# Seven-product pairs chained in two PSUM banks with held tails, three adds a pair, four weight splits, and closing products in two stretches of k tiles

## The chip, the cores and the metric

One program runs on one NeuronCore of a Trainium2 chip. The metric is the device time of one execution in microseconds (us); lower is better. The engines are TensorE (PE), VectorE (DVE), ScalarE (ACT), GpSimd (POOL) and SyncE (SP, which issues most transfers). Each works through its own queue in order and waits on semaphores for the others.

## The reference

One layer of a trunk for 128 context and 512 latent tokens (640 columns in all), width 1024, in fp32. Cut to what matters here:

```python
def swiglu(h, w_gate, w_up, w_down):
    return (jax.nn.silu(h @ w_gate) * (h @ w_up)) @ w_down      # inner width 2816

def trunk_layer(x, mod, ...):
    h = modulate(rms_norm(x, norm_ffn1), sh1, sc1)
    x = x + 0.5 * gt1 * swiglu(h, w_ffn1_gate, w_ffn1_up, w_ffn1_down)
    h = modulate(rms_norm(x, norm_mix), sh2, sc2)
    x = x + gt2 * mixer(h, ...)    # sigmoid gates; Fourier and gated linear attention branches; @ w_out
    h = modulate(rms_norm(x, norm_ffn2), sh3, sc3)
    x = x + 0.5 * gt3 * swiglu(h, w_ffn2_gate, w_ffn2_up, w_ffn2_down)
```

## The kernel before

Activations lie transposed, 128 channels on the partitions and 640 tokens along the row, cut in halves of `NH` = 320. Every fp32 operand is split in a high and a low part: `split` has ACT write the high part (L107) and DVE the rest (L108), and each product of two tiles becomes three matmuls (high by high, high by low, low by high).

**Pairs.** The gate and up projections of both FFNs, the mixer's branch gates and the projection of the attention output go through `Pair7`: a pair of 128-wide output tiles by two halves of 320 tokens, as a 2x2 scheme with seven products of half size in place of eight. Product i takes weights i, which are a quarter of the raw tile or a sum of quarters, and one of seven sums of activations that `Act7` has made. The four weight sums are made in place by POOL (L474, L477, L481, L485); `weights` splits seven pieces of 128x512. `product` runs 12 matmuls of 320 columns (L502) into a PSUM bank of its own. A `Take` object puts the seven products together: one copy on ACT (L529) and seven adds on DVE (L530 to L545). `done` of a gate pair applies silu (L556), that of an up pair multiplies on POOL (L566) and splits the result into a page of the hidden activation.

**Buffers.** `wraw` has two raw weight tiles, `wspl` ten blocks for split weights, `pb` six PSUM banks. A split waits until the last matmul that read its block is through; a transfer waits until POOL and the splits have left the raw tile.

**Stages, in order.** FFN1: an entry (three plain products and one pair, the pair's sums of activations made meanwhile by DVE and POOL, L436 and L440), then pairs in four parts of 4, 6, 6, 6 hidden tiles; after each part `down` (`gemm_w`, L138) adds its share of the down projection, one pair into the next part. Until about 325 us the weights of the modulation are streamed between the pairs (L214). The last part goes through `halved` (L392): eight output tiles by two halves, each a run over all k tiles, with the norm that follows hooked behind each tile. Then the mixer: an entry with two plain gate products (their sigmoids, `first_gate`, L1096, free the PSUM banks), a `turn` of transposes (L1045, copies L1048), gate pairs; Fourier and attention; `plain` (L1216), the branch's projection by pairs (`TakeY`), and `halved` with w_out. FFN2 is as FFN1, without the stream.

A scheduler decides at build time in which order each engine's queue holds the instructions; it is shown below from the built programs.

## Time and profile before

| | before |
|---|---|
| median of 3 runs | 1557.94 us (1556.88 to 1559.18) |
| the profiled execution | 1558.36 us, span 1556.6 us |
| mean granted TensorE clock | 0.984 |
| PE, DVE, ACT, POOL busy | 96%, 71%, 44%, 28% |
| instructions | 28126, of which 11162 matmuls |

The span is the time from the first to the last instruction on the core; some 1.8 us of the execution lie around it. The clock of 0.984 is a mean: 1 is 2.4 GHz, and 0.5 is 1.2 GHz, the lower of the two levels.

### The profile page before, as it was taken

How to read it: one execution, taken by the hardware profiler on the slowest of the kernel's cores; microseconds unless marked ns; L12 is line 12 of the kernel's file. 1: busy time of each engine (PE TensorE's matmuls, PEld its weight loads, DVE VectorE, ACT ScalarE, POOL GpSimd, SP SyncE). 2: the span in 40 equal slices, each digit the busy share in tenths (PEclk: the TensorE clock that was granted, in tenths of full speed). 3: DMA queues.
4: the chain of work that ended last, by engine and by line, in shares of the span. 5: the costliest groups of instructions: out<-in, count | busy, mean ns of one | idle time of the engine just before them, and what ended most of it. 6: DMA issues, size and time to landing. Idle time of an engine off the chain costs nothing.

```text
span 1556.6 us, 28126 instructions
## 1 busy us (share of the span) xinstructions
PE 1495.9 (96%) x11162; PEld 1457.1 (94%) x11162; DVE 1098.4 (71%) x2027; ACT 689.6 (44%) x1397; POOL 432.2 (28%) x320
## 2 busy tenths in 40 slices
PE   6989999999999999999989998989989999999998
PEld 5889999999999899999979998989989999999997
DVE  6876764675577876666668868887787674674676
ACT  5533342343345555464545454335643442442344
POOL 2432431441440000001054424310253532532510
PEclk7999999999999999999999999999999999999999
DMA  9383563522134512213124336354213222222232
GB/s 360 108 299 123 186 238 119 190 68 96 55 108 145 158 41 76 68 45 109 51 68 133 95 107 208 107 197 162 83 55 109 82 82 82 82 82 83 75 102 108
DMA packets 149338, 184.61 MB, mean 119 GB/s; under 512 B 4735, under 2 KB 121847, under 8 KB 149207
## 3 DMA queue, kind: packets, MB, share of 16 engines
q1 hardware_dynamic: 149207, 182.81, 35.7%
q8 instruction: 88, 1.44, 0.4%
q14 instruction: 43, 0.35, 0.1%
HBM read 168.64 MB, written 14.16 MB: 117 GB/s over the span
## 4 chain that ended last, share of the span: by engine, by line
PE 75%; DVE 11%; ACT 4%; issue 4%; DMA 2%; POOL 2%; SPq 1%; POOLq 0%; ACTq 0%; DVEq 0%
PE pb L502 34%; PE pb L138 16%; PE pb L392 7%; PE mm L834 4%; DVE wspl L108 3%; PE mm L138 2%; DVE pg L108 2%; PE sc L983 2%; PE sm L214 2%; ACT wspl L107 1%; DMA wraw<-in_w_in_dram 1%; PE sm L834 1%; PE pb L130 1%; ACT pg L107 1%; PE sm L1013 1%
## 5 line engine op out<-in xcount | busy, mean ns | idle before, releaser
L502 PE MATMUL pb<-pg,wspl 128*128 128x320 f32 x4452 | 667.2, 311 | 20.3 <-ACT g L1096 6.3
L502 PEld LDWEIGHTS pb<-pg,wspl 128*128 128x128 f32 x4452 | 658.2, 189 | 25.8 <-DVE wspl L108 6.9
L108 DVE TENSOR_TENSOR wspl<-wraw,wspl 128x512 fp32r<-128x512 f32 (+1 forms) x619 | 459.1, 759 | 235.3 <-ACT wspl L107 234.4
L107 ACT ACTIVATE wspl<-wraw 128x512 fp32r<-128x512 f32 (+1 forms) x619 | 359.3, 603 | 475.3 <-PE pb L138 155.3
L138 PE MATMUL pb<-pg,wspl 128*128 128x320 f32 x1920 | 288.8, 311 | 5.2 <-DVE pg L1216 5.0
L138 PEld LDWEIGHTS pb<-pg,wspl 128*128 128x128 f32 x1920 | 284.0, 189 | 6.9 <-DVE pg L1216 5.6
L474 POOL TENSOR_TENSOR wraw<-wraw 128x512 f32<-128x512 f32 x53 | 72.3, 1364 | 354.5 <-DVE wspl L108 352.0
L392 PE MATMUL pb<-pg,wspl 128*128 128x320 f32 (+2 forms) x960 | 149.8, 315 | 8.9 <-ACT pg L107 8.5
L392 PEld LDWEIGHTS pb<-pg,wspl 128*128 128x128 f32 x960 | 143.8, 192 | 10.5 <-ACT pg L107 9.4
L481 POOL TENSOR_TENSOR wraw<-wraw 128x512 f32<-128x512 f32 x53 | 69.8, 1318 | 165.4 <-DVE wspl L108 165.4
L108 DVE TENSOR_TENSOR pg<-t,pg 128x640 fp32r<-128x640 f32 (+2 forms) x64 | 60.3, 950 | 40.3 <-ACT pg L107 39.7
L834 PE MATMUL mm<-wspl,pg 128*128 128x256 f32 x672 | 87.8, 286 | 0.1
L107 ACT ACTIVATE pg<-t 128x640 fp32r<-128x640 f32 (+2 forms) x64 | 41.7, 663 | 100.6 <-POOL t L566 91.5
L834 PEld LDWEIGHTS mm<-wspl,pg 128*128 128x128 f32 x672 | 82.4, 191 | 0.7 <-ACT pg L936 0.4
L477 POOL TENSOR_TENSOR wraw<-wraw 128x512 f32<-128x512 f32 x53 | 81.9, 1546 | 4.1
L566 POOL TENSOR_TENSOR t<-t,g 128x640 f32<-128x640 f32 x40 | 63.7, 1605 | 63.0 <-DVE t L540 56.6
L485 POOL TENSOR_TENSOR wraw<-wraw 128x512 f32<-128x512 f32 x53 | 70.5, 1331 | 4.2
L372 DVE SCALAR_TENSOR_TENSOR pg<-pb,hg,pg 128x320 f32<-128x320 f32 x144 | 54.4, 433 | 19.0 <-PE pb L138 19.0
L1035 POOL TENSOR_TENSOR rs<-ms,negh 128x5 f32<-128x5 f32 x4 | 4.8, 1200 | 206.9 <-DVE ms L1033 206.9
L108 DVE TENSOR_TENSOR pg<-pg,pg 128x320 fp32r<-128x320 f32 (+2 forms) x80 | 58.3, 775 | 0.2 <-ACT pg L107 0.2
L138 PE MATMUL mm<-pg,wspl 128*128 128x320 f32 x288 | 52.3, 326 | 0.0
L130 PE MATMUL pb<-pg,wspl 128*128 128x320 f32 x288 | 47.2, 321 | 4.2 <-ACT wspl L107 2.9
(211 smaller groups left out, 1542.0 us busy)
## 6 DMA issues: line engine op xcount, KB each, us to landing
pg<-in_w_ada_dram SPq DMA_DIRECT2D x72, 512.0 KB, 7.5
wraw<-in_w_ffn_down_dram SPq DMA_DIRECT2D x32, 768.0 KB, 4.6
wraw<-in_w_ffn_gate_dram SPq DMA_DIRECT2D x22, 1024.0 KB, 5.2
wraw<-in_w_ffn_up_dram SPq DMA_DIRECT2D x22, 1024.0 KB, 5.2
wraw<-in_w_in_dram SPq DMA_DIRECT2D x22, 512.0 KB, 3.8
wraw<-in_w_in_dram SPq DMA_DIRECT2D x10, 1024.0 KB, 5.1
wraw<-in_w_out_dram SPq DMA_DIRECT2D x8, 1024.0 KB, 5.5
gbd<-g SPq DMA_DIRECT2D x16, 320.0 KB, 2.4
```

The lines of the kernel that those rows point to most:

```text
L107: S.activation(out=hi, in_=src, func=AF.Copy)
L108: eng.tensor_tensor(out=lo, in0=src, in1=hi.bitcast(F32), op=ALU.subtract)
L130: T.matmul(out=bank(ps, hf)[:, 0:NH], lhsT=w[a][k], rhs=acts[k][:, b, hf * NH:(hf + 1) * NH], start=(k == 0 and ti == 0), stop=(k == nk - ...
L138: T.matmul(out=bank(ps, hf)[:, 0:NH], lhsT=w[a][k], rhs=acts[k][:, b, hf * NH:(hf + 1) * NH], start=(k == 0 and ti == 0), stop=(k == nk - ...
L392: T.matmul(out=ps[:, 0:c1 - c0], lhsT=w[a][i], rhs=acts[i][:, b, c0:c1], start=(i == 0 and ti == 0), stop=(i == nk - 1 and ti == 2))
L474: G.tensor_tensor(out=self.a11, in0=self.a11, in1=self.a21, op=ALU.subtract)
L477: G.tensor_tensor(out=self.a21, in0=self.a21, in1=self.a22, op=ALU.add)
L481: G.tensor_tensor(out=self.a22, in0=self.a22, in1=self.a11, op=ALU.subtract)
L485: G.tensor_tensor(out=self.a12, in0=self.a12, in1=self.a22, op=ALU.subtract)
L502: T.matmul(out=self.p[i], lhsT=self.w[i][:, s, k, :], rhs=x[k][:, t, :], start=(k == 0 and ti == 0), stop=(k == self.n - 1 and ti == 2))
L566: G.tensor_tensor(out=x, in0=x, in1=g, op=ALU.mult)
L834: T.matmul(out=ps_out, lhsT=h2[k][:, a, t * P:(t + 1) * P], rhs=w[b][k], start=(k == 0 and ti == 0), stop=(k == KD - 1 and ti == 2))
```

## The change

A pair's products go into two banks that accumulate several products each: product 1 opens bank A, and 6, 7 and 4 are added to it by the matmuls themselves; product 5 opens bank B, and 3 is added to it; product 2 has a bank of its own. Between two products ACT copies what the bank holds so far (`p1`, `p16`, `p167`). Three adds on DVE are left (`p2`, `p5`, `p53`). The order of a pair is now 1, 2, 6, 5, 7, and its products 3 and 4 are held back (`held`) until the next pair: 3 runs behind that pair's 2, and 4 behind its 5. Where no pair follows, `flush_pair` runs them behind the first product of what comes next.

Weights are split in three pieces of 128x1024 (weights 1 and 2; 7 and 5; 6 and 3) and one of 128x512 (4), in four double blocks (`wspl2`) and two single ones, which take the room that the ten had. All other splits of weights go in pieces of up to 1024 too. A pair's sums stand in two steps: two sums, the split of 7 and 5, two sums, the split of 6 and 3.

`halved` runs the first four tiles of its first half over all k tiles but the last two, runs the held tails behind the first of them, and then closes the four. At the two FFN entries and the mixer's entry the calls for weights and activation sums stand in another order.

```diff
-NBLK = 10
+NBLK = 2
+NBLK2 = 4
...
+    def block2():
+        uid[0] += 1
+        return wspl2.tile([P, 2, 1024], F32R, tag="wspl2", name=f"wsplb{uid[0]}")
+
-    def wsplit(src, new=block, room=512):
+    def wsplit(src, new=block2, room=1024):
...
         for hf, c0, c1 in ((0, 0, cut), (1, cut, N)):
+            opened = []
             for mp in range(4):
                 rd = load(wd, r0, nk, mp * 256, 256)
                 for m in range(2):
                     w = wsplit(rd[:, :, m * P:(m + 1) * P])
...
+                    ps = pb_ps()
+                    if hf == 0 and mp < 2:
+                        some(ps, w, c0, c1, range(nk - 2))
+                        opened.append((2 * mp + m, ps, w))
+                        flush_pair()
+                        continue
+                    some(ps, w, c0, c1, range(nk))
+                    close(2 * mp + m, ps, hf, c0, c1)
+                if mp == 1:
+                    for k, ps, w in opened:
+                        some(ps, w, c0, c1, range(nk - 2, nk))
+                        close(k, ps, hf, c0, c1)
...
+            if i in (1, 2):
+                self.double(self.raw[:, :, 0:P], 1, 2, whole)
+            elif i in (5, 7):
+                self.weights(1)
+                G.tensor_tensor(out=self.a11, in0=self.a11, in1=self.a21, op=ALU.subtract)
+                G.tensor_tensor(out=self.a21, in0=self.a21, in1=self.a22, op=ALU.add)
+                self.double(self.raw[:, self.ks[0], :], 7, 5, lambda j, o: (j, o * P))
+            elif i in (6, 3):
+                self.weights(7)
+                G.tensor_tensor(out=self.a11, in0=self.a22, in1=self.a11, op=ALU.subtract)
+                G.tensor_tensor(out=self.a12, in0=self.a12, in1=self.a11, op=ALU.subtract)
+                self.double(self.raw[:, :, 0:P], 6, 3, whole)
...
         def begin(self):
-            self.product(1)
-            self.product(2)
-            self.take.c11(self.p[1], self.p[2])
+            self.A, C = pb_ps()[:, 0:NH], pb_ps()[:, 0:NH]
+            self.product(1, self.A, True)
+            self.take.p1(self.A)
+            self.product(2, C, True)
+            self.take.p2(C)
+            flush_step()
 
         def end(self):
-            self.product(7)
-            self.product(4)
-            self.product(6)
-            self.take.uv(self.p[6], self.p[7])
-            self.take.c21(self.p[4])
-            self.product(5)
-            self.take.c22(self.p[5])
-            self.product(3)
-            self.take.c12(self.p[3])
+            self.product(6, self.A, False)
+            self.take.p16(self.A)
+            self.B = pb_ps()[:, 0:NH]
+            self.product(5, self.B, True)
+            flush_step()
+            self.product(7, self.A, False)
+            self.take.p167(self.A)
+            self.take.p5(self.B)
+            held.extend((self.tail3, self.tail4))
...
+        def p16(self, ps):
+            self.w = sm_tile([P, NH], "sqh")
+            S.activation(out=self.w, in_=ps, func=AF.Copy)
...
+        def p53(self, ps):
+            self.last = V.tensor_tensor(out=self.x0[:, NH:N], in0=self.w, in1=ps, op=ALU.add)
+            self.done(0)
...
                 pd = out_ps()
                 gemm_w(pd, w, hid)
+                flush_pair()
...
-                    pair.sum(5)
+                    pair.weights(7)
                     act.each(act.sum4)
-                    pair.weights(7)
+                    act.each(act.put2)
+                    pair.weights(6)
+                    pair.begin()
+                    act.each(act.put1)
+                    t = swiglu(p[2], pu)
+                    keep(t, hid)
                     act.each(act.put4)
                     pair.weights(4)
...
             pair.weights(7)
-            act.each(act.put4)
-            pair.weights(2)
+            act.each(act.put2)
+            pair.weights(6)
         first_gate(m)
     turn()
+    pair.begin()
+    act.each(act.put1)
+    act.each(act.put4)
     pair.weights(4)
-    pair.begin()
-    act.each(act.put2)
-    pair.weights(6)
-    act.each(act.put1)
-    pair.weights(5)
     pin(m2)
     pair.end()
```

ACT's queue at the mixer's entry, before: from the split of weights 7 (`wspl_8620`) to the sigmoids of the second gate product (L1096); `pg_` are splits of activation sums.

```order
L107 ACTIVATE wspl_8620<-wraw_8494 128x512
L107 ACTIVATE pg_8470<-pg_8454 128x320
L107 ACTIVATE pg_8470<-pg_8455 128x320
L107 ACTIVATE pg_8471<-pg_8456 128x320
L107 ACTIVATE pg_8471<-pg_8457 128x320
L107 ACTIVATE wspl_8631<-wraw_8494 128x512
L1096 ACTIVATE g_8634<-pb_8566 128x320
L1096 ACTIVATE g_8634<-pb_8567 128x320
```

The same place of the changed kernel: `wsplb_8184` is the split of weights 7 and 5, `wsplb_8197` that of 6 and 3, L1161 the sigmoids.

```order
L109 ACTIVATE wsplb_8184<-wraw_8057 128x1024
L109 ACTIVATE pg_8035<-pg_8023 128x320
L109 ACTIVATE pg_8036<-pg_8024 128x320
L109 ACTIVATE pg_8037<-pg_8025 128x320
L109 ACTIVATE pg_8038<-pg_8026 128x320
L109 ACTIVATE wsplb_8197<-wraw_8057 128x1024
L1161 ACTIVATE g_8200<-pb_8129 128x320
L1161 ACTIVATE g_8200<-pb_8130 128x320
```

The sigmoids stood behind a split of raw weights 2; they now stand behind that of 6 and 3, which needs all four sums of the pair.

PE's queue at the entry of FFN2, before: the end of product 2 of the first pair (`wspl_12099`), product 7 (`wspl_12173`) and the start of product 4 (`wspl_12184`).

```order
L502 MATMUL pb_12214<-pg_11602,wspl_12099 128x320 x3
L502 MATMUL pb_12251<-pg_12074,wspl_12173 128x320 x3
L502 MATMUL pb_12251<-pg_12075,wspl_12173 128x320 x3
L502 MATMUL pb_12251<-pg_12076,wspl_12173 128x320 x3
L502 MATMUL pb_12251<-pg_12077,wspl_12173 128x320 x3
L502 MATMUL pb_12264<-pg_12078,wspl_12184 128x320 x6
```

Now: the end of product 2 (`wsplb_11398`), product 6 (`wsplb_11485`, the split of 6 and 3) and the start of product 5 (`wsplb_11468`).

```order
L537 MATMUL pb_11489<-pg_10931,wsplb_11398 128x320 x3
L537 MATMUL pb_11488<-pg_11376,wsplb_11485 128x320 x3
L537 MATMUL pb_11488<-pg_11377,wsplb_11485 128x320 x3
L537 MATMUL pb_11488<-pg_11378,wsplb_11485 128x320 x3
L537 MATMUL pb_11488<-pg_11379,wsplb_11485 128x320 x3
L537 MATMUL pb_11561<-pg_10885,wsplb_11468 128x320 x3
```

The third product of the entry's pair is now one whose weights need all four sums; before it was one that needs the first alone.

POOL's queue in FFN2 between a gate pair and an up pair, before: the sums of the up pair's weights (`wraw_13128`, L474 and L477, L481 and L485) and the two multiplications of the up pair ahead of it (L566).

```order
L474 TENSOR_TENSOR wraw_13128<-wraw_13128 128x4x128
L477 TENSOR_TENSOR wraw_13128<-wraw_13128 128x4x128
L566 TENSOR_TENSOR t_12893<-t_12893,g_12501 128x640
L566 TENSOR_TENSOR t_12892<-t_12892,g_12500 128x640
L481 TENSOR_TENSOR wraw_13128<-wraw_13128 128x4x128
L485 TENSOR_TENSOR wraw_13128<-wraw_13128 128x4x128
```

Now, for an up pair (`wraw_12578`) in the same place: sums L517, L518, L522, L523, multiplications L629 (half a row) and L634.

```order
L629 TENSOR_TENSOR t_12354<-t_12354,g_12229 128x320
L517 TENSOR_TENSOR wraw_12578<-wraw_12578 128x4x128
L634 TENSOR_TENSOR t_12353<-t_12353,g_12228 128x640
L518 TENSOR_TENSOR wraw_12578<-wraw_12578 128x4x128
L522 TENSOR_TENSOR wraw_12578<-wraw_12578 128x4x128
L523 TENSOR_TENSOR wraw_12578<-wraw_12578 128x4x128
```

The whole-row multiplication now stands between the first and the second sum; the split of 7 and 5 needs both.

## Rows read from the trace of the kernel before

**Rows 1.** Page, busy time by engine: us, share of the span, instructions.

```profile
PE 1495.9 (96%) x11162; PEld 1457.1 (94%) x11162; DVE 1098.4 (71%) x2027; ACT 689.6 (44%) x1397; POOL 432.2 (28%) x320
```

**Rows 2.** The chain of waits by time: start, us, what ran.

```profile
1205.32 73.92 PE pb L502 x504
```

**Rows 3.** Waits of PE: line, awaited engine and line, us in total, times, longest.

```profile
PE pb L392 <- ACT pg L107: 8.5, 3, 3.9
PE pb L502 <- ACT g L1096: 6.3, 1, 6.3
PE pb L502 <- DVE wspl L108: 5.5, 4, 1.8
PE pb L138 <- DVE pg L1216: 5.0, 2, 4.6
PE pb L502 <- ACT g L578: 3.4, 2, 2.1
PE pb L502 <- DVE hn L533: 3.2, 2, 2.9
```

**Rows 4.** Windows, PE alone: window, us, busy us (instructions), granted clock, DMA share, GB/s.

```profile
464.00:472.00 8.00, 5.67 (x39) 1.00 0.33 100
809.60:813.60 4.00, 3.97 (x15) 0.52 0.74 250
850.00:858.00 8.00, 5.06 (x24) 0.79 0.46 139
961.00:971.00 10.00, 5.01 (x21) 0.66 0.13 44
1037.00:1050.00 13.00, 8.72 (x38) 0.74 0.87 320
```

**Rows 5.** Groups by form: line, shapes, count, busy us, mean ns, idle before.

```profile
L108 DVE TENSOR_TENSOR wspl<-wraw,wspl 128x512 fp32r<-128x512 f32 x555 | 426.1, 785 | 233.7 <-ACT wspl L107 233.0 <-issue 0.3
L107 ACT ACTIVATE wspl<-wraw 128x512 fp32r<-128x512 f32 x555 | 333.8, 625 | 441.1 <-PE pb L138 141.7 <-POOL wraw L481 106.1 <-PE pb L502 72.1
L533 DVE TENSOR_TENSOR hn<-hn,pb 128x320 f32<-128x320 f32 x53 | 25.5, 480 | 17.3 <-PE pb L502 17.2
L529 ACT ACTIVATE hn<-pb 128x320 f32<-128x320 f32 x53 | 22.6, 426 | 15.6 <-PE pb L502 15.5
L942 DVE TENSOR_TENSOR pg<-pg,pg 128x1280 f32<-128x1280 f32 x4 | 6.0, 1493 | 23.9 <-ACT pg L941 23.9
L941 ACT ACTIVATE pg<-pg 128x1280 f32<-128x1280 f32 x4 | 5.1, 1274 | 0.1
L474 POOL TENSOR_TENSOR wraw<-wraw 128x512 f32<-128x512 f32 x53 | 72.3, 1364 | 354.5 <-DVE wspl L108 352.0 <-DVE mod L221 2.5
L477 POOL TENSOR_TENSOR wraw<-wraw 128x512 f32<-128x512 f32 x53 | 81.9, 1546 | 4.1
L566 POOL TENSOR_TENSOR t<-t,g 128x640 f32<-128x640 f32 x40 | 63.7, 1605 | 63.0 <-DVE t L540 56.6 <-DVE t L545 4.2 <-ACT wspl L107 2.2
```

**Rows 6.** Timelines of PE, POOL and DVE at the mixer's entry: start, us, work, idle before.

```profile
809.63 6.67 PE L502 MATMUL pb<-pg,wspl 128*128 128x320 f32 x32 [6.27 <-ACT g L1096]
...
799.11 6.30 POOL L440 TENSOR_TENSOR pg<-pg 128x320 f32<-128x320 f32 x4 [3.05 <-DVE pg L436]
...
806.72 1.27 POOL L477 TENSOR_TENSOR wraw<-wraw 128x512 f32<-128x512 f32 x1
812.60 1.76 POOL L481 TENSOR_TENSOR wraw<-wraw 128x512 f32<-128x512 f32 x1 [4.62 <-DVE wspl L108]
...
801.70 1.36 DVE L108 TENSOR_TENSOR wspl<-wraw,wspl 128x512 fp32r<-128x512 f32 x1
...
810.06 0.68 DVE L108 TENSOR_TENSOR wspl<-wraw,wspl 128x512 fp32r<-128x512 f32 x1
```

**Rows 7.** Timelines of PE and POOL at the entry of FFN2.

```profile
1133.52 3.68 PE L502 MATMUL pb<-pg,wspl 128*128 128x320 f32 x24
...
1133.36 4.51 POOL L440 TENSOR_TENSOR pg<-pg 128x320 f32<-128x320 f32 x4 [2.37 <-DVE pg L436]
```

More of the change, by code (lines that the diff above doesn't have):

```diff
@@ L373, in add_gated, with halved @@
                                    in1=X[k][:, a:b], op0=ALU.mult, op1=ALU.add)
-    def halved(wd, r0, acts, gate, X, each, mid, cut=NH):
-        nk = len(acts)
+    def halved(wd, r0, nk, acts, gate, X, each, mid, cut=NH):
         late = []
@@ L381, in flush, with some, close @@
                 late.pop(0)()
+        def some(ps, w, c0, c1, ks):
+            for i in ks:
+                for ti, (a, b) in enumerate(((0, 0), (0, 1), (1, 0))):
+                    T.matmul(out=ps[:, 0:c1 - c0], lhsT=w[a][i], rhs=acts[i][:, b, c0:c1],
+                             start=(i == 0 and ti == 0), stop=(i == nk - 1 and ti == 2))
+        def close(k, ps, hf, c0, c1):
+            flush()
+            for r, a, b in ((0, c0, min(c1, NL)), (1, NL, c1)):
+                if a < b:
+                    V.scalar_tensor_tensor(out=X[k][:, a:b], in0=ps[:, a - c0:b - c0], scalar=gate[:, k, r:r + 1],
+                                           in1=X[k][:, a:b], op0=ALU.mult, op1=ALU.add)
+            late.append(lambda: each(k, hf))
+            if hf == 1 and k in mid:
+                late.append(mid[k])
         for hf, c0, c1 in ((0, 0, cut), (1, cut, N)):
+            opened = []
             for mp in range(4):
@@ L489, in weights, with product @@
                 return
-            self.sum(i)
-            self.w[i] = self.block()
-            src = {1: self.a11, 2: self.a12, 3: self.a12, 4: self.a22, 5: self.a21, 6: self.a22, 7: self.a11}[i]
-            split(self.w[i][:, 0], self.w[i][:, 1], src)
-        def product(self, i):
+            whole = lambda j, o: (range(2 * self.n)[self.ks[o]][j], 0)
+            if i in (1, 2):
[10 more added lines that the diff above has]
+                self.double(self.raw[:, :, 0:P], 6, 3, whole)
+            else:
+                t = block()[:, :, 0:self.n * P]
+                v = [t[:, s].rearrange("p (k c) -> p k c", k=self.n) for s in range(2)]
+                split(v[0], v[1], self.a22)
+                self.w[4] = [[v[s][:, j, :] for j in range(self.n)] for s in range(2)]
+        def product(self, i, bank, first):
             self.weights(i)
@@ L549, in out, with p1674, p53 @@
             return [sm_tile([P, N], self.tag) for _ in range(2)]
-    class TakeGate(Take):
+    class TakeAct(Take):
         tag = "g"
+        def p1674(self, ps):
+            S.activation(out=self.x1[:, 0:NH], in_=ps, func=self.func)
+            S.activation(out=self.x1[:, NH:N], in_=self.x1[:, NH:N], func=self.func)
+            self.done(1)
+        def p53(self, ps):
+            self.last = V.tensor_tensor(out=self.x0[:, NH:N], in0=self.w, in1=ps, op=ALU.add)
+            S.activation(out=self.x0, in_=self.x0, func=self.func)
+            self.done(0)
+    class TakeGate(TakeAct):
+        func = AF.Silu
         def done(self, i):
-            x = self.x1 if i else self.x0
-            S.activation(out=x, in_=x, func=AF.Silu)
+            pass
     class TakeUp(Take):
@@ L652, in ffn @@
             if f0 + nf == DFF // P:
-                halved(wd, f0 * P, hid, gate, X, each, mid, cut)
+                halved(wd, f0 * P, nf, hid, gate, X, each, mid, cut)
                 break
```

147 lines of the change are left out of this document (65 added, 82 removed).

## The prediction

> **What bounds the kernel now.** The page comes first: PE is busy for 1495.9 us of the span [rows 1], and no other engine comes near. The chain of waits tells what undisturbed work costs: 504 matmuls of a pair's kind in 73.92 us [rows 2], or 0.147 us each. A product of 12 is 1.76 us, a pair of 84 is 12.3 us. The change leaves the number of matmuls alone (seven products of 12 for each pair, the closing tiles only cut in two), so time can come or go only where PE waits or runs at the lower clock. The waits of PE name the places [rows 3]; the windows show where the clock fell beside them [rows 4].
>
> The reader is to see two things there. Inside the FFN stages there is no wait of weight on the list: all named ones lie at entries and at closings. And the clock falls after some waits and not after others: 464 to 472 us, with a wait of 2.3 us, keeps 1.00, while the windows round the waits of 2.9, 3.9, 4.6 and 6.3 us show 0.52 to 0.79. At 0.52 PE is at 1.2 GHz nearly throughout. I take it that a wait of up to 2.3 costs itself, and one from 2.9 up about 2 us more.
>
> **What the change should give.** *Closings (L392).* Three waits, 8.5 us, the longest 3.9 [rows 3], so the other two are 2.3 each. The two of 2.3 lie at the FFN closings, the long one at w_out. In the changed kernel PE has, when it gets there, the first tile over all but two k tiles, then the held products 3 and 4 (3.5 us), then three tiles more before it needs the last two. With six k tiles these three are 3 x 12 matmuls = 5.3 us, with w_out's eight 3 x 18 = 7.9 us. That is more than each wait. At w_out the clock goes back too: 0.74 over 13 us is 3.4 us lost [rows 4]. 2.3 + 2.3 + 3.9 + 3.4 = 11.9, and I take 11.5, since the last hidden tiles now come later by the held products. The last sums there are not on the list of anything else.
>
> *The wait for `plain`'s add (L1216).* 4.6 us of its 5.0, with the clock at 0.66 over 10 us. That is 3.4 us by the window, but PE worked only half of it, so about 2 is real. The held products of the gate pair put 3.5 us of PE work ahead of it and the rest, about 1.1, is too short for a fall. Gain 3.5 + 2 = 5.5.
>
> *The wait for the add L533 among the gate pairs.* 2.9 us, and 0.79 over 8 us, which is 1.7 us. DVE is what is late here. It loses four adds of 0.48 us a pair [rows 5], 1.9 us, and the splits get no dearer. Most of 4.6 should go: 3.5.
>
> Sum of the gains: 20.5 us.
>
> **What each new operation costs.** A DVE split of 1024 columns isn't in the trace. From below: the two-input instruction of 1280 columns, 1.49 us [rows 5], by 1024/1280 is 1.19. From above: two splits of 512 at the slowest row, 1.36 each [rows 6], or 2.7. I take 1.22, near the lower end, since an undisturbed 512 is 0.68 [rows 6] and the longer instruction saves one start. On ACT the bounds are 1.02 (1.27 for 1280) and 1.25 (two of 0.625) [rows 5]; I take 1.06. The two new copies of a bank are 0.43 each, as L529; ACT is busy for 44% [rows 1] and hides them, unless they stand behind something that waits (below). Per pair DVE goes from 7 x 0.785 + 7 x 0.48 = 8.9 us to some 3 x 1.22 + 0.785 + 3 x 0.48 = 5.9. It is hidden work in the FFN stages, so worth nothing there by itself. Of the other splits in larger pieces I expect nothing either way: the attention stage has no wait of PE on the list that a split ends. Bounds: 2 us more or less.
>
> **What it should take.** *Mixer's entry.* PE now waits 6.27 us for the second gate's sigmoids and goes on at 809.63 [rows 6]. These now stand behind the split of 6 and 3, as the order shows. POOL ends the activation sums at 799.11 + 6.30 = 805.4; two weight sums of 1.27 take it to 808.0; the split of 7 and 5 ends at 809.1 on ACT and 810.3 on DVE; two more sums 812.9; the split of 6 and 3 on ACT 814.0; two sigmoids at some 0.4, 814.8. Product 1 then starts 5.2 us later than now. The clock has fallen already now, so no more is lost by it. I count 5.2.
>
> *Both FFN entries.* Now they cost PE 5.5 + 3.4 us together (the waits for L108's blocks and for L578) [rows 3], 4.45 each. In the new order product 6 is third. In FFN2 products 1 and 2 end at 1133.52 + 3.68 = 1137.2, POOL's activation sums at 1133.36 + 4.51 = 1137.9 [rows 7]. Behind these stand the last two weight sums, 2.8 us, and the split: ACT 1141.8, DVE 1143.0, which the third matmul needs. PE waits 5.8 us in place of 4.45, and that is long enough for a fall of the clock, which now doesn't come: 4.0 us at 0.52 [rows 4] lose 1.9. So 3.2 more at each, 6.4 for both, if FFN1's entry goes as FFN2's.
>
> *The FFN pairs.* A block of 1 and 2 comes free when product 2 ends, and from there runs a chain: ACT split 1.06, DVE 1.22, the two sums 1.36 and 1.55 [rows 5], ACT split of 7 and 5 1.06. Where an up pair is followed by a gate pair, ACT's queue has the copy `p16` of the running pair behind that split, and product 7 waits for the copy: 0.43 more, 6.7 in all with 0.1 for the start 6.8. PE in that time has products 3, 6, 5 and 4, 7.04 us. It fits by 0.2. But in the cycle before, POOL does the whole-row multiplication, 1.6 us [rows 5], between the two sums (the order above). The up pair's split of 6 and 3 then ends on ACT at 12.9 us after the gate pair's product 2, past the end of the up pair's own product 2 at 12.3; the next split starts 0.6 late on ACT, and is 1.1 late on DVE, where that of 6 and 3 (1.22) comes first. Less the slack of 0.2, product 7 is some 0.9 to 1.0 late. There are eight such places that neither the modulation's stream nor a down projection covers (two in FFN1, six in FFN2): 8 us.
>
> Sum of the losses: 5.2 + 6.4 + 8 = 19.6 us.
>
> **The sum.** The profiled execution took 1558.36 us, 0.4 above the median. 1558.4 - 20.5 + 19.6 = 1557.5; as to the median, about 1557. The two large sums cancel; each has its own uncertainty.
>
> **The rivals.**
> *The chain fits* (0.32). If the splits of 7 and 5 and of 6 and 3 take their lower bounds and the sums the undisturbed 1.27 [rows 6], the delay in the cycle before shrinks by about 0.9 and product 7 waits for nothing. For it: in the FFN stages PE waits for nothing now, and DVE has a third less to do. Against: the order puts three engines in one chain with 0.2 us of slack. The 8 us are not paid: 1549.
>
> *The chain is too long for every pair* (0.20), the other side. POOL and DVE slow each other when both work: L481 took 1.76 at 812.60 against 1.27 undisturbed, and a split on DVE 1.36 against 0.68 [rows 6]. If the DVE split of 1024 comes to 1.9, half way to double, both on the way (1 and 2; 6 and 3) add 0.7, so the eight places pay 2.4 each, 19 us, and eight transitions with no multiplication between pay about 0.5, 4 us. That is 15 more than the forecast: 1572. It decides from a split of about 1.5. The Trainium skill, page "SBUF — State Buffer", section "Who interferes with whom", says that VectorE and GpSimd share one pair of ports as an exclusive lock, so that an instruction of the one holds off the other to its end; a split with two SBUF inputs is of that kind, and a longer one would hold POOL's sums for longer. The rows of contention agree with it; how far a piece of 1024 is hit no run here shows yet.
>
> *The held work does not fill the waits* (0.10). If the held products come to a place where the engine behind them was late anyway, the results that the closings wait for are late by the same 3.5 us, and only half of the 20.5 comes: 1567.
>
> **How the numbers follow.** The forecast itself, the cancelling, has 0.38 and a range of its own of 1551 to 1563 (the terms are good to some 3 us each). 0.2%, about what a measurement of this kernel can tell from no change, is 3.1 us, so 1554.8 to 1561.1 counts as no change. Faster: the first rival 0.32 and 0.10 of the forecast's 0.38. No change: 0.20 of it. Slower: its last 0.08, and the other two rivals with 0.30. The range of 1546 to 1576 goes 3 below the first rival and 4 above the second.
>
> **What would show it.** Right: PE's waits at the two FFN closings gone, and the one at w_out gone with its window back at 1.00; the wait at the mixer's entry longer, some 11 us, still ended by the sigmoids (L1161); at the FFN entries a wait of near 6 us for the split of 6 and 3; in FFN2 waits of about 1 us ahead of product 7, ended by the copy L582, and DVE near a third less busy. Wrong: no waits at L582, or many more than eight; a split of 1024 above 1.5 us on DVE; a wait at the closings that comes back as one for the held products' results; a gate stage that still waits for DVE.

## Result and the profile after

The changed kernel takes 1597.26 us (median of 4, 1594.64 to 1598.31) against 1557.41 for the kernel before: 1.0254 times as long [1.0235, 1.0274]. The forecast was 1557, with a range up to 1576. The profiled execution is the one of 1598.31 us, with a span of 1596.5 us, a mean granted clock of 0.977 and 27071 instructions.

The page first, its line of busy times:

```profile
PE 1507.8 (94%) x11162; PEld 1463.5 (92%) x11162; DVE 995.3 (62%) x1544; ACT 692.4 (43%) x1253; POOL 419.0 (26%) x320
```

The number of matmuls is unchanged, DVE is busy for 9% less [rows 1] where the forecast looked for near a third, and PE is busy for 12 us more in a span 40 us longer: it ran longer at the lower clock and it waited more. PE's waits, the longest groups:

```profile
engine line waited for: us in total, times, longest us
PE pb L537 <- ACT hn L575: 13.7, 3, 6.0
PE pb L537 <- ACT g L1161: 12.0, 1, 12.0
PE pb L537 <- DVE g L589: 11.7, 11, 3.1
...
PE pb L537 <- ACT sqh L582: 5.0, 3, 2.3
PE pb L537 <- ACT wsplb L109: 3.4, 3, 1.9
PE pb L391 <- DVE wsplb L110: 3.4, 1, 3.4
```

L537 is `product`, as L502 was. Of the waits of before [rows 3], those for L533, for `plain`'s add and at the closings are gone, but one closing has a new one (L391), and `plain` has one of 2.3 us for L611 (below). In their place stand waits for ACT's copies, and eleven for the add L589 (`p5`).

The starts of PE's work in both traces give the account by place, in us. The 24 matmuls of held products that move over a boundary are put back at 0.147 each; `plain` begins with its first product.

| place | forecast | measured |
|---|---|---|
| FFN1 entry | +3.2 | +14.5 |
| FFN1 pairs | +2 | +4.0 |
| FFN1 closing | -2.3 | +3.6 |
| attention stage | 0 | -1.6 |
| mixer entry | +5.2 | +5.7 |
| gate pairs | -3.5 | +1.1 |
| `plain` | -5.5 | -3.3 |
| projection by `TakeY` | 0 | +9.3 |
| closing at w_out | -6.9 | -7.4 |
| FFN2 entry | +3.2 | +6.7 |
| FFN2 pairs | +6 | +8.4 |
| FFN2 closing | -2.3 | -0.8 |
| sum | -0.9 | +40.2 |

**`plain`.** Behind its first product and the held ones PE waits for L611, the add `p53` of the held product 3, and the clock falls with it. PE's timeline, then the window (us, busy times of PE, PEld, DVE, ACT and POOL, granted clock):

```profile
987.14 22.89 PE L144 MATMUL pb<-pg,wsplb 128*128 128x320 f32 x144 [2.29 <-DVE g L611]
```

```profile
987.20:990.60 3.40, 3.40 (x13) 3.40 (x14) 3.24 (x4) 3.40 (x8) 2.81 (x3) 0.50 0.40 93
```

**FFN2 pairs.** The chain of waits of after, one transition from an up pair to a gate pair (start, length, what):

```profile
1357.75 12.33 PE pb L537 x84
...
1370.11 1.07 ACT wsplb L109
...
1371.20 1.24 DVE wsplb L110
...
1372.51 1.30 POOL wraw L517
1373.81 1.53 POOL t L634
1375.35 1.27 POOL wraw L518
...
1376.64 1.07 ACT wsplb L109
...
1377.73 1.23 DVE wsplb L110
1378.96 0.40 DVE t L628
1379.36 1.17 DVE wspl L110
...
1380.80 1.92 DVE pg L110
1382.72 0.41 DVE g L589
...
1383.17 12.60 PE pb L537 x83
```

When PE leaves a block, ACT and DVE split 1024 columns, POOL does a sum, the multiplication L634 and a second sum, ACT and DVE split again, and DVE does the split of 512 and that of the hidden activation before the add L589. Only then may product 3 go on in bank B: 1383.17 - 1370.08 = 13.1 us, where PE has 12.3 us of work. Every such transition costs 0.8.

**FFN1 entry.** SP's timeline, the transfers that it issues, of before and then of after:

```profile
80.78 12.03 SPq L197 DMA_DIRECT2D pg<-in_w_ada_dram  x11
92.90 1.44 SPq L103 DMA_DIRECT2D wraw<-in_w_ffn_gate_dram  x1
```

```profile
87.24 22.18 SPq L203 DMA_DIRECT2D pg<-in_w_ada_dram  x15
109.52 1.87 SPq L105 DMA_DIRECT2D wraw<-in_w_ffn_gate_dram  x1
```

The next gate tile is fetched 16.6 us later, behind four more transfers of the modulation. ACT's timeline of after, and then PE's, show who waits:

```profile
118.77 1.06 ACT L109 ACTIVATE wsplb<-wraw 128x1024 fp32r<-128x1024 f32 x1 [7.20 <-DMA wraw<-in_w_ffn_gate_dram]
```

```profile
77.92 11.22 PE L537 MATMUL pb<-pg,wsplb 128*128 128x320 f32 x60 [5.79 <-ACT hn L575]
...
116.21 3.15 PE L220 MATMUL sm<-pg,cs 128*32 128x128 f32 x64 [4.14 <-DMA pg<-in_w_ada_dram]
```

**FFN2 entry.** PE's timeline; the wait of 5.95 is the one worked out as 5.8, and a second of 1.87 stands 14 us behind it:

```profile
1169.10 14.10 PE L537 MATMUL pb<-pg,wsplb 128*128 128x320 f32 x75 [5.95 <-ACT hn L575]
1185.07 4.88 PE L537 MATMUL pb<-pg,wsplb 128*128 128x320 f32 x21 [1.87 <-ACT wsplb L109]
```

The windows show where the clock fell to 1.2 GHz; two more of the falls, neither behind a long wait:

```profile
1021.30:1024.70 3.40, 3.08 (x11) 3.09 (x12) 1.20 (x1) 0.26 (x1) 2.05 (x2) 0.50 0.00 0
...
1185.20:1188.60 3.40, 3.40 (x13) 3.40 (x14) 2.30 (x2) 1.50 (x2) 0.37 (x1) 0.50 0.35 76
```

They stand beside the waits of 2.29 us (below) and 1.87, as the one in `plain` does beside its 2.29: a wait of under 2.3 us, which I had taken to cost only itself, can bring one. The kernel before shows it too: its clock is 0.50 from 110.3 to 113.7 us, behind a wait of 1.68 that ends at 108.18.

**Projection by `TakeY`.** PE's timeline, then ACT's: a copy takes 0.42 us, but stands in ACT's queue behind a split that waits for POOL's sum.

```profile
1015.55 3.78 PE L537 MATMUL pb<-pg,wsplb 128*128 128x320 f32 x24 [2.00 <-ACT hn L575]
1021.62 12.22 PE L537 MATMUL pb<-pg,wsplb 128*128 128x320 f32 x72 [2.29 <-ACT sqh L582]
```

```profile
1020.18 1.06 ACT L109 ACTIVATE wsplb<-wraw 128x1024 fp32r<-128x1024 f32 x1 [4.69 <-POOL wraw L518]
1021.14 0.42 ACT L582 ACTIVATE sqh<-pb 128x320 f32<-128x320 f32 x1
```

### The profile page after: what moved, and what is told of

Same layout as the page of the kernel before. It is cut to its first block, busy times and chain, and to the rows that moved or that the text cites. A ratio compares the mean times of both kernels' runs of the same rounds, so it can differ in the third digit from the quotient of the medians.

```text
span 1596.5 us, 27071 instructions
## 1 busy us (share of the span) xinstructions
PE 1507.8 (94%) x11162; PEld 1463.5 (92%) x11162; DVE 995.3 (62%) x1544; ACT 692.4 (43%) x1253; POOL 419.0 (26%) x320
## 4 chain that ended last, share of the span: by engine, by line
PE 70%; DVE 12%; POOL 7%; ACT 5%; issue 3%; DMA 2%; POOLq 0%; SPq 0%; ACTq 0%; DVEq 0%
PE pb L537 30%; PE pb L144 13%; PE pb L391 8%; PE mm L901 5%; DVE wsplb L110 4%; ACT wsplb L109 3%; DVE pg L110 3%; PE mm L144 2%; PE sc L1050 2%; PE sm L220 2%; POOL wraw L518 2%; POOL wraw L517 2%; PE sm L901 2%; PE pb L136 1%; DVE wspl L110 1%
## 5 line engine op out<-in xcount | busy, mean ns | idle before, releaser
L537 PE MATMUL pb<-pg,wsplb 128*128 128x320 f32 x3816 | 595.7, 315 | 49.3 <-ACT hn L575 13.7
L537 PEld LDWEIGHTS pb<-pg,wsplb 128*128 128x128 f32 x3816 | 574.1, 192 | 61.6 <-ACT hn L575 14.8
L109 ACT ACTIVATE wsplb<-wraw 128x1024 fp32r<-128x1024 f32 (+2 forms) x295 | 286.8, 976 | 428.6 <-PE pb L144 131.1
L110 DVE TENSOR_TENSOR wsplb<-wraw,wsplb 128x1024 fp32r<-128x1024 f32 (+2 forms) x295 | 340.9, 1158 | 208.3 <-ACT wsplb L109 205.6
L144 PE MATMUL pb<-pg,wsplb 128*128 128x320 f32 x1920 | 289.3, 311 | 2.4 <-DVE g L611 2.3
L144 PEld LDWEIGHTS pb<-pg,wsplb 128*128 128x128 f32 x1920 | 284.3, 189 | 3.6 <-issue 2.7
L517 POOL TENSOR_TENSOR wraw<-wraw 128x512 f32<-128x512 f32 x53 | 70.4, 1329 | 449.6 <-DVE wsplb L110 449.6
L391 PE MATMUL pb<-pg,wsplb 128*128 128x320 f32 (+2 forms) x960 | 149.1, 314 | 3.4 <-DVE wsplb L110 3.4
L391 PEld LDWEIGHTS pb<-pg,wsplb 128*128 128x128 f32 x960 | 143.9, 192 | 3.8 <-DVE wsplb L110 3.6
L522 POOL TENSOR_TENSOR wraw<-wraw 128x512 f32<-128x512 f32 x53 | 72.4, 1366 | 128.6 <-DVE wsplb L110 128.6
L537 PE MATMUL pb<-pg,wspl 128*128 128x320 f32 x636 | 102.4, 309 | 0.6 <-ACT hn L586 0.6
L537 PEld LDWEIGHTS pb<-pg,wspl 128*128 128x128 f32 x636 | 95.5, 188 | 1.0 <-ACT hn L586 0.8
L901 PE MATMUL mm<-wsplb,pg 128*128 128x256 f32 x672 | 87.2, 286 | 0.0
L109 ACT ACTIVATE pg<-t 128x640 fp32r<-128x640 f32 (+1 forms) x56 | 40.9, 730 | 103.2 <-POOL t L634 61.0
L901 PEld LDWEIGHTS mm<-wsplb,pg 128*128 128x128 f32 x672 | 82.4, 191 | 0.4 <-ACT pg L1003 0.2
L523 POOL TENSOR_TENSOR wraw<-wraw 128x512 f32<-128x512 f32 x53 | 80.3, 1515 | 4.2
L518 POOL TENSOR_TENSOR wraw<-wraw 128x512 f32<-128x512 f32 x53 | 72.0, 1359 | 3.2
L110 DVE TENSOR_TENSOR wspl<-wraw,wspl 128x512 fp32r<-128x512 f32 x53 | 64.9, 1224 | 9.6 <-ACT wspl L109 9.4
```

Of the source, the lines that this page charges most:

```text
L109: S.activation(out=hi, in_=src, func=AF.Copy)
L110: eng.tensor_tensor(out=lo, in0=src, in1=hi.bitcast(F32), op=ALU.subtract)
L144: T.matmul(out=bank(ps, hf)[:, 0:NH], lhsT=w[a][k], rhs=acts[k][:, b, hf * NH:(hf + 1) * NH], start=(k == 0 and ti == 0), stop=(k == nk - ...
L391: T.matmul(out=ps[:, 0:c1 - c0], lhsT=w[a][i], rhs=acts[i][:, b, c0:c1], start=(i == 0 and ti == 0), stop=(i == nk - 1 and ti == 2))
L517: G.tensor_tensor(out=self.a11, in0=self.a11, in1=self.a21, op=ALU.subtract)
L518: G.tensor_tensor(out=self.a21, in0=self.a21, in1=self.a22, op=ALU.add)
```

## The experiments

The theory after the result: the weights of a pair now pass through one chain of ACT, DVE and POOL that is about as long as PE's pair, and longer wherever other work stands in it. So a loss of PE isn't made up, and what is put right in one place shows only where the chain lets it. A ratio is to the kernel before in the same job; "the changed kernel" is the 1597.26 above. The kernel before had medians of 1554.4 to 1557.4 us in these jobs, so a difference in us between jobs is good to some 3 us.

**e1_gate_first.** The sigmoids of the mixer's second gate ahead of the split of 6 and 3.

```diff
         else:
             pair.weights(7)
             act.each(act.put2)
+            first_gate(m)
             pair.weights(6)
-        first_gate(m)
+        if m == 0:
+            first_gate(m)
```

> The second gate's sigmoids are called ahead of the split of weights 6 and 3, nothing else is changed. Theory of the queues (what PE waits for stands on ACT behind a split that needs all four weight sums): the wait of 11.97 us at the mixer's entry falls to 6 to 7 us and the time by 4 to 6 us, to some 1592. Rival (the pair's weights are the limit there whatever the order): product 6 then waits for the same split, the loss moves by two products, and the time falls by less than 2.

1596.39 us, 1.0269 [1.0254, 1.0285]. The wait is halved and the first product starts at 829.38 in place of 835.58. PE's timeline shows where the 6.2 us go:

```profile
829.38 5.28 PE L537 MATMUL pb<-pg,wsplb 128*128 128x320 f32 x24 [6.62 <-ACT g L1161]
836.07 11.32 PE L537 MATMUL pb<-pg,wsplb 128*128 128x320 f32 x74 [1.41 <-ACT hn L575]
...
852.20 1.00 PE L537 MATMUL pb<-pg,wsplb 128*128 128x320 f32 x5 [2.98 <-ACT wsplb L109]
...
865.60 0.56 PE L537 MATMUL pb<-pg,wsplb 128*128 128x320 f32 x2 [2.37 <-ACT hn L575]
```

By 893 us it is where the changed kernel is, to 0.5 us. The rival holds: behind the entry, the chain sets the pace.

**e2_w4_early.** At the FFN entries, the split of weights 4 where it was before the change, so that the raw tile comes free early.

```diff
                     t = swiglu(p[0], p[1])
                     pair.weights(1)
+                    pair.weights(4)
...
                     act.each(act.put4)
-                    pair.weights(4)
```

> At both FFN entries the split of weights 4 is called right behind that of 1 and 2, not behind the last activation sums. SyncE's queue then has the next gate weights' transfer ahead of the modulation's transfers, as the kernel before had it nearly. Theory of the queues: the waits of PE from 104 to 127 us (0.6, 4.1, 0.5, 0.3, 1.0, 0.7) and the two falls of the clock there go, the time falls by 7 to 11 us. Rival (the transfers together are the limit in this stretch): the modulation's transfers land later instead and the time falls by less than 3.

1582.76 us, 1.018 [1.0163, 1.0197]: 14.5 us less, some 12 by the ratios. Over FFN1's first three pairs PE takes 60.7 us in place of 73.9 (53.9 before, to which 3.5 are to be added for the 24 matmuls of the down projection that stand among them now); the gate's transfer stands ahead of the modulation's again. PE gets to FFN1's closing at 468.3 in place of 480.3. So 12 us of FFN1's entry are the place of one transfer in SP's queue.

**e3_entry_sums.** Weight sums first, activation sums 4 last, at the FFN entries.

```diff
-                    act.each(act.sum2)
                     pair.weights(7)
-                    act.each(act.sum4)
-                    act.each(act.put2)
+                    act.each(act.sum2)
                     pair.weights(6)
+                    act.each(act.put2)
                     pair.begin()
+                    act.each(act.sum4)
```

> At both FFN entries the split of 7 and 5 is called ahead of the activation sums of product 6, and the split of 6 and 3 ahead of those of product 4. Theory of the queues: the wait of product 6 (5.8 and 5.95 us) falls by 3 to 4 at each entry, the clock no longer falls there, and the time comes down by 7 to 11 us. Rival (DVE and POOL hold each other off, so that the sums only change places): the wait falls by 1 or less at each, 3 us in all.

1596.02 us, 1.0264 [1.0244, 1.0283]. The waits at L575 fall from 13.7 to 8.8 us, those at L109 rise from 3.4 to 6.8, and the next pairs give the rest back. As in e1, no gain.

**e4_tail_swap.** Product 4 behind the next pair's product 2, and 3 behind its 5, which gives the add L589 three products more.

```diff
-            held.extend((self.tail3, self.tail4))
+            held.extend((self.tail4, self.tail3))
...
         def p1674(self, ps):
...
-            self.hid += self.h
...
         def done(self, i):
...
+            self.hid += self.h
```

> The two held products change places: 4 runs behind the next pair's 2, and 3 behind its 5. Theory: the 13 waits of 13.7 us for the add L589 are product 3 waiting for bank B to be read, so with 3.5 us more they go, and the time falls by 8 to 11 us. Rival (blocks): the split of 7 and 5 now waits for the block that product 3 frees 3.5 us later, product 7 waits for the copy behind that split, and the time stays within 3 us or rises by up to 15.

1619.92 us, 1.0414 [1.0392, 1.0437]: 23 us more than the changed kernel. The waits at L589 are gone, but the double block of weights 6 and 3 is held longer, and the splits come late:

```profile
PE pb L537 <- ACT hn L575: 26.8, 15, 6.0
PE pb L537 <- DVE wsplb L110: 12.8, 26, 0.7
```

The rival (the blocks) has the direction, but the loss is larger than the 15 us that it allowed.

**e5_no_sums.** Leaves POOL's four weight sums out, so products 3, 5, 6 and 7 take the raw quarters.

```diff
-                G.tensor_tensor(out=self.a11, in0=self.a11, in1=self.a21, op=ALU.subtract)
-                G.tensor_tensor(out=self.a21, in0=self.a21, in1=self.a22, op=ALU.add)
...
-                G.tensor_tensor(out=self.a11, in0=self.a22, in1=self.a11, op=ALU.subtract)
-                G.tensor_tensor(out=self.a12, in0=self.a12, in1=self.a11, op=ALU.subtract)
```

> The four weight sums of every pair are left out (POOL's L517, L518, L522, L523), so products 3, 5, 6 and 7 take the raw quarters; nothing else is changed. Theory of one chain per pair (split 1.06 on ACT and 1.23 on DVE, two sums 2.7, split, two sums 2.7, split: some 12.3 us, as long as PE's 12.3 us for a pair, so that no pair catches up a delay): without its 5.4 us of sums the waits among the gate pairs, in the projection of the attention output and at L589 in the FFNs go, and the time falls by 25 to 45 us. Rival (the queues' order and the held products are what PE waits for): it falls by less than 10.

A single execution took 1532.8 us: 64 less than the changed kernel, more than expected. No wait of a pair is on the list but the sigmoids' 2.4 us. Two groups by form, of after and then of e5 (mean ns of one):

```profile
L110 DVE TENSOR_TENSOR wspl<-wraw,wspl 128x512 fp32r<-128x512 f32 x53 | 64.9, 1224 | 9.6 <-ACT wspl L109 9.4
L110 DVE TENSOR_TENSOR pg<-t,pg 128x640 fp32r<-128x640 f32 x52 | 60.3, 1162 | 10.3 <-ACT pg L109 10.1
```

```profile
L110 DVE TENSOR_TENSOR wspl<-wraw,wspl 128x512 fp32r<-128x512 f32 x53 | 36.5, 688 | 58.3 <-ACT wspl L109 58.2
L110 DVE TENSOR_TENSOR pg<-t,pg 128x640 fp32r<-128x640 f32 x52 | 42.6, 822 | 12.7 <-ACT pg L109 12.5
```

The sums cost twice: they stand in the chain, and they hold DVE's small splits off. The Trainium skill, page "SBUF — State Buffer", section "Who interferes with whom", says that a VectorE instruction with two SBUF inputs contends with a GpSimd one that reads SBUF; the 688 ns without sums and 1224 with them agree.

**e9_sums_junk.** POOL does the same four sums at the same places, but no split waits for them.

```diff
+    sumj = const.tile([P, 4, P], F32, name="sumj")
...
-                G.tensor_tensor(out=self.a11, in0=self.a11, in1=self.a21, op=ALU.subtract)
+                G.tensor_tensor(out=sumj[:, 0:self.n, :], in0=self.a11, in1=self.a21, op=ALU.subtract)
```

(and so for the other three; a page less, for the room).

> POOL makes the four weight sums of every pair at full size, but writes them to a spare tile, and the products take the raw quarters, as without sums; 28 pages make room for the tile. So POOL still works beside DVE, and no split waits for it. Theory (what counts is that the splits wait for the sums, in one chain a pair): the time is near that without sums, 1530 to 1545. Rival (what counts is that POOL and DVE hold each other off): 1560 or more, with waits at L589 left.

A single execution took 1584.33 us: only 13 less than the changed kernel, which is the rival's range. From FFN2's fourth pair on, at the projection by `TakeY` up to 1 us, and at the first mixer pair's start, PE goes as in e5: there the chain is the cause. In FFN1's first pairs, in the gate pairs and in FFN2's entry it stays slow. In FFN1's second and third part four pairs take 16.1 to 19.1 us, where the changed kernel takes 13.3 to 14.4: a loss of e9's own. DVE's split of 1024 takes 1398 ns against 1231 in the changed kernel, since it now runs beside the sums. Both causes exist; with a page less, their shares can't be told.

**e10_sums_dve.** The four sums on DVE.

```diff
-                G.tensor_tensor(out=self.a11, in0=self.a11, in1=self.a21, op=ALU.subtract)
+                V.tensor_tensor(out=self.a11, in0=self.a11, in1=self.a21, op=ALU.subtract)
```

(and so for the other three).

> The changed kernel with all four weight sums on DVE, 0.68 us each in place of 1.3 to 1.5 on POOL. Theory of the chain: it gets 2.6 us shorter a pair, delays are caught up, DVE's pieces of 512 and 640 columns go back to 0.68 and 0.82, and the time falls by 30 to 50 us, to 1550 to 1565, though DVE has 2.7 us more work a pair. Rival (DVE becomes what is waited for, 2.7 us a pair being more than it gets back): the time stays above 1580, with waits for adds on DVE.

1559.32 us, 1.0016 [1.0003, 1.0028]: 38 us back with the same chain of steps. The group by form of the first sum shows why (DVE):

```profile
L517 DVE TENSOR_TENSOR wraw<-wraw 128x512 f32<-128x512 f32 x53 | 37.0, 697 | 0.5
```

A sum takes 0.70 in place of 1.33 us (L518 1.01), the splits of 512 are short again (687 ns), and DVE is still only 69% busy. The waits at L589 and L582 are off the list. The Trainium skill's page "GPSIMD Engine Reference", section "Performance versus the Vector engine", puts a two-input add on GpSimd at 1.96 times VectorE's time; 1.33 to 0.70 agrees, L518's 1.36 to 1.01 does not.

**e11_sums_dve_all.** e10, e2 and e1 together. **e12_before_sums_dve.** The control: the kernel before, with its four sums (L474 to L485) on DVE.

```diff
-                G.tensor_tensor(out=self.a11, in0=self.a11, in1=self.a21, op=ALU.subtract)
+                V.tensor_tensor(out=self.a11, in0=self.a11, in1=self.a21, op=ALU.subtract)
...
+                    pair.weights(4)
...
+            first_gate(m)
```

> As e10, and the split of weights 4 called early at the FFN entries, and the sigmoids ahead of the split of 6 and 3 at the mixer's entry. Theory: with a chain that can catch up, the two local gains now last: 12 us at FFN1's entry and 4 to 6 at the mixer's, 15 to 18 us below e10, so 1533 to 1550, faster than the kernel before. Rival (the pairs still set the pace after each entry): 13 us for the first alone.

> A control: the kernel before with its four weight sums on DVE. In it a pair's products 1, 2, 7 and 4 need one sum at most, its chain has slack, and DVE has 8.9 us of work a pair already. Theory of the chain: no gain in the FFN stages, DVE late in the gate stage, the time within 10 us of 1557 or slower. Rival (POOL's sums are what costs both kernels time): faster by 10 or more.

1549.31 us, 0.9935 [0.9918, 0.9951], and 1548.9 us, 0.9933 [0.9918, 0.9948]. e11 is 10 us below e10, where 15 to 18 were expected. Both beat both kernels, and they are equal: the move of the sums is worth 8.4 us in the kernel before, and the change, with its two entries mended, adds nothing to that.

**e16_combo2.** e11 and e3 together.

```diff
-                    act.each(act.sum2)
...
+                    act.each(act.sum2)
                     pair.weights(6)
```

> As e11 (sums on DVE, split of 4 early, sigmoids first), and at the FFN entries the splits of 7 and 5 and of 6 and 3 ahead of the activation sums, as e3. Theory: with a chain that catches up, the 2.5 to 3 us that e3 won at each entry and lost again now last, and the clock falls for less: the time falls by 4 to 9 us below e11, to 1540 to 1546, faster than the kernel before with its sums on DVE. Rival (DVE is full at the entries, so that the order there only moves the wait): within 2 us of e11.

1550.72 us, 0.9961 [0.9946, 0.9975], no better than e11. Its waits at L575 come to 15.0 us against e11's 13.8; with the sums on DVE, that engine is what the entries wait for, to judge by e11's trace: at FFN2's entry DVE works with one pause of 1.2 us from 1116.7 us until its last sum ends at 1131.3, and only then come the split and the copy that PE waits for until 1132.8.

**e13_p16_first.** The copy `p16` ahead of the split of 7 and 5 in ACT's queue: the step that the forecast named for the FFN pairs.

```diff
+                with tc.issue_after(copied[0].ins) if copied else nullcontext():
+                    self.double(self.raw[:, self.ks[0], :], 7, 5, lambda j, o: (j, o * P))
...
-            S.activation(out=self.w, in_=ps, func=AF.Copy)
+            copied[:] = [S.activation(out=self.w, in_=ps, func=AF.Copy)]
```

> The changed kernel with the split of 7 and 5 placed behind the copy p16 of the pair ahead of it in ACT's queue, everywhere. The prediction put its 8 us for the FFN pairs on that copy standing behind that split. If that is the cause, the time falls by 6 to 10 us. Theory now (the pair's chain as a whole is as long as PE's pair, and PE meets it at product 3, waiting for the add L589, in nine places and at the copy in three): the three waits of 5.0 us at L582 go, others grow by as much, and the time stays within 3 us.

1591.56 us, 1.0221 [1.0201, 1.0241]. The waits at the copy are off the list, those at the add (L591 here) stand at 12.2 us in 11 places, and over FFN2's pairs PE needs 375.3 us in place of 376.9. The time fell by 5 to 6 us, more than the theory's 3 and less than the 6 to 10 of the forecast's cause; of the 5.2 between the profiled executions, 2.9 lie before the first pair, where the edit changes nothing. The copy is a small part.

**e6_singles.** Ten single blocks and seven splits of 512 a pair, with the new order of products. **e14_singles_p16** adds e13's edit to it.

```diff
-NBLK = 2
-NBLK2 = 4
+NBLK = 10
...
-    def wsplit(src, new=block2, room=1024):
+    def wsplit(src, new=block, room=512):
...
+                part = src[:, ks[0]:ks[-1] + 1, c0:c0 + P]
+                t = block()[:, :, 0:self.n * P]
+                v = [t[:, s].rearrange("p (k c) -> p k c", k=self.n) for s in range(2)]
+                split(v[0], v[1], part)
```

> The four splits are undone alone: ten single blocks as before, each of the seven weights split by itself (512 columns), all other splits of 512 too; the two banks, the held products, the sums in two steps and the closings stay. Theory of one chain per pair: ACT and DVE overlap within a step, each of the three steps gets some 0.9 us shorter and blocks come free one by one, the time falls by 15 to 35 us. Rival (the sums in two steps and the order are the whole of it): within 5 us of the changed kernel; a second rival, that more instructions make DVE late, has it slower.

> Ten single blocks (as e6, which was 75 us slower than the changed kernel), with the same ordering of the copy p16 ahead of the splits of 7 and 5. Theory: with finer blocks the queue put up to five splits ahead of the copy, two of them waiting for the last sums; without that the 46.8 us of waits at the copy go, and the time falls by 40 to 75 us, to 1600 to 1630. Rival (the finer splits themselves, 12 pieces more a pair through ACT and DVE, cost the time): it falls by less than 15.

1672.28 us, 1.0744 [1.0721, 1.0768], and 1699.46 us, 1.0916 [1.0888, 1.0944]. My theory that finer steps shorten the chain fell twice. In e6 PE waits most for the copy, in e14 for the add L586 (42.9 us in one group and 25.0 in a second); the longest group of PE's waits in e6:

```profile
PE pb L532 <- ACT sqh L577: 46.8, 25, 4.9
```

So the copy's place in ACT's queue is not what makes e6 slow; what does stays open. Nor does any run go back to a bank for each product, so what the two banks cost by themselves is not known. One thing is shown: e6 and e14 have no wait at the closing of FFN1.

**e7_no_hold.** Products 3 and 4 at once, at the end of their own pair.

```diff
-            held.extend((self.tail3, self.tail4))
+            self.tail3()
+            self.tail4()
```

> Products 3 and 4 run at the end of their own pair. Theory: product 3 then waits for the copy and the add of bank B (0.44 + 0.49 us behind product 7), about 1 us at each of 53 pairs, and the closings lose their cover, so the time rises by 30 to 60 us. Rival (holding keeps the block of 6 and 3 until after the next pair's product 2, and so holds up the next splits): the chain starts 5 us earlier, and the time falls by 10 or more in spite of these waits.

1627.37 us, 1.0456 [1.0436, 1.0476]: the holding back is worth 30 us, the low end of the expectation. The reason expected, a wait of about 1 us behind product 7 in each of 53 pairs, is not on the list: the copy `p167` is waited for 9 times, 4.6 us in all, and the longest group is the copy `p1`, 24.7 us in 11 places.

**e8_blocks5.** Five double blocks, paid for with two pages.

```diff
-NPAGES = 29
+NPAGES = 27
...
-NBLK2 = 4
+NBLK2 = 5
```

> A fifth double block; to make room there are 27 pages in place of 29. Theory: the split of 1 and 2 no longer waits for product 2 of the pair before, so two chains overlap and delays are caught up: the waits at L589, L582 and L575 outside the entries go, the time falls by 15 to 30 us. Rival (the chain is bound by ACT, DVE and POOL standing in line and not by blocks): less than 5.

1624.76 us, 1.0443 [1.0422, 1.0463]: 27 more, and the theory that the four blocks are the limit fell. The rival had no such rise either. PE waits 23.8 us at L575 (9 times) and 20.0 at L589. That splits issued further ahead stand before the copies in ACT's queue is only argued; the pages may count as well. At the closing of FFN1 the wait at L391 is 2.1 us in place of 3.4.

**e15_one_stretch.** The closing tiles in one run over all k tiles, as before, with the held products ahead of them.

```diff
+        flush_pair()
         for hf, c0, c1 in ((0, 0, cut), (1, cut, N)):
-            opened = []
...
-                    if hf == 0 and mp < 2:
-                        some(ps, w, c0, c1, range(nk - 2))
-                        opened.append((2 * mp + m, ps, w))
-                        flush_pair()
-                        continue
```

> The two stretches of the closings are undone: the held products run first, then all tiles over all k tiles, as before. Theory (the stretches and the held products fill the waits there): the waits of 2.3, 3.9 and 2.3 us come back, with up to 1 us more each for the products that now come right before, and the fall of the clock at w_out; without the wait of 3.4 us in FFN1's closing, which stands behind four closings at once on DVE. The time rises by 7 to 13 us. Rival (only w_out's gains): it rises by 3 to 6.

1597.6 us, 1.0265 [1.0244, 1.0287], no change. The closings' waits for the hidden splits are 1.5 us in all, against 8.5 before [rows 3]. My theory that the two stretches hide them fell for the FFN closings. At w_out PE's queue as built still has 39 closing matmuls ahead of the wait, where a tile has 24, so there the stretches are not undone; the closing takes 0.8 us longer.

## Why the prediction was wrong

**"If FFN1's entry goes as FFN2's"** failed, by 11 us. The wait is the expected one (5.79), but the split of weights 4 went to the end, so the raw tile came free late and its next transfer was issued behind four more of the modulation's. e2 gives 12 us back. The forecast counted the engines' queues at this place, not SP's.

**Gains and losses were summed as if PE resumed its pace after each stall.** A pair's weights are now a chain, in which ACT's queue alone keeps each split behind the sums of the one before: sums 1.33 + 1.36, ACT 1.06, DVE 1.23, sums 1.37 + 1.52, ACT 1.06, DVE 1.23 twice, 11.4 us a pair by the means of the groups by form. PE's pair is 12.3, and other work stands in the chain: the multiplication of 1.53 makes 12.9 of it in the FFN pairs, where 13.1 is measured. In the `TakeY` stage the chain of waits of after shows a cycle of 13.85 us from one L517 to the next, most of it DVE's:

```profile
1030.99 1.30 POOL wraw L517
...
1035.25 1.23 DVE wsplb L110
1036.48 0.75 DVE pg L110
...
1039.06 1.71 DVE wspl L110
1040.76 0.75 DVE pg L110
...
1043.63 1.15 DVE wsplb L110
...
1044.84 1.31 POOL wraw L517
```

So what is late stays late, or grows. This is the largest gap, 13.9 us: the gate pairs (+1.1 for -3.5) and the `TakeY` projection (+9.3 for 0), where I had no term. e1 and e3 show it from one side (a wait removed comes back), e5 and e10 from the other (with a shorter chain 64 and 38 us less). These two also free DVE from running beside POOL's sums; e9 shows the waiting for sums alone to be the cause in FFN2's pairs from the fourth on and, to 1 us a pair, at `TakeY`; elsewhere the shares stay open. The term for L533 failed with it: DVE had less to do, but the adds now wait behind splits that wait for sums, and the 2.9 us for L533 have come back as 3.1 for L589: the gate stage that still waits for DVE, a sign of being wrong that the forecast had named.

**The FFN pairs** were sized at two thirds, 8 for 12.4, with the right chain, POOL's multiplication in it. The end of that chain was wrong: product 3 waits for the add L589, not product 7 for the copy, as e13 and the chain of waits show.

**Rival 2** (too long for every pair) had the direction. Its premise did not hold: the split of 1024 came to 1.23, as priced. What grew is the split of 512, which I had at 0.785 and which came to 1.22 (0.69 in e5, without sums). That of the hidden activation takes 1.16, about as before the change (1.12), against 0.82 in e5.

**`plain`.** The 4.6 us were to shrink to 1.1, too short for a fall of the clock. PE waits 2.29 us, for the result of a held product, and the clock falls for 3.4 us: -3.3 for -5.5. The third rival had named such a wait, though at the closings.

**Closings.** At w_out -7.4 for -6.9, but the mechanism is only in part the one forecast. Without the two stretches (e15) the waits at the FFN closings are 0.7 us each: the last split that they need is ready 2.0 and 3.0 us after the last product, against 4.4 before, so there the shorter work behind that product does most of it. At w_out it is 5.4 against 7.5, and what the stretches add there e15 does not tell. At FFN1's closing a new wait of 3.4 us and a fall of the clock took the gain. A split there can be issued only when PE leaves a block. DVE is then within the norm's work, from 519.81 almost without a pause, and gets to it at 526.22:

```profile
525.63 0.67 DVE L398 SCALAR_TENSOR_TENSOR pg<-pb,hg,pg 128x192 f32<-128x192 f32 x2
526.22 0.95 DVE L110 TENSOR_TENSOR wsplb<-wraw,wsplb 128x768 fp32r<-128x768 f32 x1
```

The wait goes with the number of blocks: 3.4 us with four double ones, 2.1 with five (e8, with two pages less), none with ten single ones (e6, e14). I had expected "nothing either way" of the other splits in larger pieces.

**Right:** the mixer's entry (a wait of 12.0 by the sigmoids, worked out at 11; +5.7 for +5.2), and the wait at the FFN entries (5.95 for 5.8). At FFN2's entry the second wait and its fall of the clock were missed.

## What to carry to other kernels

Before adding up the waits that a change removes, add up the new chain of one cycle over all engines and compare it with the bound engine's cycle: when the two are about equal, nothing lost is won back, and a wait taken away in one place comes back in the next. When a step that frees a buffer is moved, follow the transfer that reuses it into its DMA queue. And when a change comes out slower, run its best ingredient on the old kernel too: here the sums on DVE gave 8.4 us there, all that the mended new one had.

## What the runs showed of the hardware

DVE's splits of 512 took 1224 ns in the kernel with POOL's sums and 688 without them (e5), while those of 1024 took 1231 against 1261: POOL mostly waits for them then. In e9, where it doesn't, they take 1398. The penalty falls on whatever happens to run beside POOL. And two waits of 2.29 us and one of 1.87 each stood beside a fall of 3.4 us to 1.2 GHz (987.2, 1021.3 and 1185.2), while one of 2.00 that ends at 1015.55 had none right behind it, nor had those of 2.3 at the FFN closings before the change [rows 4]. The length of a wait alone does not tell whether the clock falls.
